# Two-layer hybrid encoder on one Trainium2 core: the first feed-forward product of 19 of 22 column pairs as seven products of quarters, with all sums of weights on VectorE

## The chip, the cores and the metric

The kernel runs on one core of a Trainium2 chip. The core has a matrix engine (TensorE, PE in the profile; PEld is its weight load), a vector engine (VectorE, DVE), a scalar engine (ScalarE, ACT), a general one (GpSimd, POOL) and a queue that issues transfers (SyncE, SP). The engines run side by side, each its own list of instructions in order, and wait for each other by semaphores. The metric is the device time of one execution in microseconds. Each kernel is timed in several runs, and the median counts.

## What is computed

Two layers of an encoder over 512 tokens with 1024 features in float32. Each layer mixes the tokens with four kinds of mixers (gated linear attention, neighbourhood attention, a linear recurrence, dilated attention) and then applies a gated feed-forward part of width 2816:

```python
for l in range(DEPTH):                       # DEPTH = 2
    h = rmsnorm(x, mix_norm_pre[l])
    p = h @ w_in[l]
    ...                                      # four mixers on slices of p, joined to y (512 x 1024)
    x = x + rmsnorm(y, mix_norm_post[l])
    h = rmsnorm(x, ffn_norm_pre[l])
    gate, up = jnp.split(h @ ffn_w_in[l], 2, axis=-1)        # 1024 x 5632 weights
    f = (jax.nn.silu(gate) * up) @ ffn_w_out[l]              # 2816 x 1024 weights
    x = x + rmsnorm(f, ffn_norm_post[l])
```

The change concerns `h @ ffn_w_in[l]` alone, the first feed-forward product.

## The kernel before, in words

**Products.** TensorE multiplies in a rounded float32 format. To keep float32 precision every operand is split into a high part (a cast, `wh` for weights) and a low part (the rest, `wl`), and `mm3` (L357) issues three matmuls into one accumulator: high by high, high by low, low by high. For the first feed-forward product the weights are the stationary operand, so the first two share `wh`, the third takes `wl`, and the activations stream, 512 columns (tokens) at a time.

**The first feed-forward product**, `ffn_in` (L1288). The 5632 output features are 22 column pairs: pair i holds 128 gate features and the 128 up features that belong to them. Pairs 0 to 2 (`NP`) are run by `parts` in two cuts of 256 tokens, so that they can start while the later tokens are still being normalised. Pairs 3 to 21 are run one after the other: for each of the two banks (a `d` bank for gate, an `x` bank for up) `mpart` (L628) issues 8 chunks of the 1024 features, three matmuls of 512 columns each, so 48 matmuls per pair. When both banks are done, `ffn_act` (L1303) makes Silu(gate) on ACT, the multiplication by up on DVE, a cast on ACT and a low part on DVE; the result `f[i]` is two tiles of 128x512, in the form the second product wants.

**The second product**, `ffn_out` (L1317), goes over k = 0 to 21 in order and uses `f[k]` and one tile of weights each, with 12 matmuls of 512 columns.

**Weights.** `w_load` (L407) walks through all weights in the order of use (`stream`, L388). It issues the transfers on SP and starts a `w_split` (L425) for each half tile: a cast on ACT and a low part on DVE or POOL, whichever is free first by the builder's reckoning. `w_get` (L442) hands them to the products in the order of use. At most four split tiles (`NW`) of this kind exist at a time; the other tiles come from a pool of 74 (`NM`, named `m`).

**What sets the order.** The program is built by a planner (`go`, L318). Every piece of work is a Python generator that yields the engine it needs next ("P", "A", "V", "G", "D"). The planner keeps a clock for each engine, advances the piece that could start first (then by the number given as its priority), and adds a modelled cost. What it emits is a fixed list of instructions for each engine. On the chip an engine runs its list in that order, so an instruction that must wait holds up all behind it on its engine, even those whose inputs are there.

All instructions of the profile below have line L187, that of the helper that records them.

Of the kernel before, what the change touches and what calls it, by code (L numbers as in the profile page):

```python
# [15 lines left out]
P = 128  # L16
L = 512
# [21 lines left out]
CUTS = ((0, 256), (256, 512))  # L39
NV = 44  # L40
# [101 lines left out]
class Timed:  # L142
# [5 lines left out]
    def __getattr__(self, name):  # L148
# [47 lines left out]
       "VP": 77, "GG": 60, "GV": 60, "GA": 75, "GP": 60}  # L196

# [7 lines left out]
class Builder:  # L205
# [151 lines left out]
    def mm3(self, out, a, b, first=True, last=True):  # L357

        mm = self.pe.matmul
        mm(out, a[0], b[0], start=first, stop=False)  # L360
        mm(out, a[0], b[1], start=False, stop=False)
        mm(out, a[1], b[0], start=False, stop=last)
# [25 lines left out]
    def stream(self):  # L388
        d = self.d
        for l in range(self.depth):  # L390
            for i in range(W2_AT):
                yield d["w1"][l, i], "m" if NW // 2 <= i < NF else "w"
            for i in range(KD // 2):
                yield d["w2"][l, i], "w"
            for i in range(W2_AT, 20):
                yield d["w1"][l, i], "w"
            for h in range(2):
                for i in range(KD // 2):
                    yield d["wo"][l, h, i], "wm"[h]
            for i in range(KF):  # L400
                for j in range(2):
                    yield d["wf1"][l, i, j], "m" if NW // 2 <= 2 * i + j < 2 * NP else "w"
            for h in range(2):
                for i in range(KF // 2):
                    yield d["wf2"][l, h, i], "m" if h and 2 * i >= KF - TAIL else "w"

    def w_load(self):  # L407
        for i, (src, kind) in enumerate(self.stream()):
# [12 lines left out]
            for h in range(2):  # L421
                self.spawn(self.w_split(2 * i + h, half[h], kind, "" if k == "s" and h == 0 else k),
                           1 if i > 2 else i - 2.5)
# [61 lines left out]
    def pre_half(self, t, i, r, gi, h, ok, keep):  # L485
# [15 lines left out]
        for k, src, g in part:  # L501
            self.act.activation(h[0][k][:, ts], src, AF.Copy, scale=g)
        yield "V"
        for k, src, g in part:
            self.dve.scalar_tensor_tensor(h[1][k][:, ts], src, g, h[0][k][:, ts].bitcast(F32), ALU.mult, ALU.subtract)
# [122 lines left out]
    def mpart(self, h, bank, c0=0, c1=L, w=None):  # L628

        new = not w  # L630
        for k in range(KD):
            if new and k % 4 == 0:
                a = yield from self.w_get()
                if w is not None:
                    w.append(a)
            elif not new:
                a = w[k // 4]
            s = slice((k % 4) * P, (k % 4) * P + P)
            if k % 2 == 0:
                yield "P"  # L640
            self.mm3(bank[:, c0:c1], (a[0][:, s], a[1][:, s]), (h[0][k][:, c0:c1], h[1][k][:, c0:c1]),
                     k == 0, k == KD - 1)
            if k % 4 == 3 and (w is None or c1 == L):
                self.give(*a[2:])
# [78 lines left out]
    def z_proj(self, l, h, st):  # L723
# [4 lines left out]
        for k in range(KD):  # L728
            if k % 2 == 0:
                yield "P"  # L730
            if k:
                self.pe.matmul(b[0:32], w[:, k * 64:k * 64 + 32], h[1][k], start=False, stop=False)
            self.pe.matmul(b[0:64], w[:, k * 64:(k + 1) * 64], h[0][k], start=k == 0, stop=k == KD - 1)
            if k == 0:
                self.pe.matmul(b[0:32], w[:, 0:32], h[1][0], start=False, stop=False)
# [13 lines left out]
    def v_proj(self, l, h, st):  # L749
# [3 lines left out]
        for k in range(KD):  # L753
            w = yield from self.w_get()
            for t in range(NT):
                if t % 2 == 0:
                    yield "P"
                a = (h[0][k][:, t * P:(t + 1) * P], h[1][k][:, t * P:(t + 1) * P])
# [460 lines left out]
    def new_h(self):  # L1219
        return [self.m(F32R) for _ in range(KD)], [self.m(F32R) for _ in range(KD)]  # L1220

# [65 lines left out]

    def ffn_in(self, l, h, ok, f):  # L1288
# [3 lines left out]

        yield from self.parts(h, ok, "dx" * NP, CUTS, done)
        for i in range(NP, KF):
            b = []
            for n in "dx":
                b.append((yield from self.acq(n)))
            for n in range(2):
                yield from self.mpart(h, b[n])
            self.spawn(self.ffn_act(i, b, f), 2)  # L1300
        self.give("m", 16)
# [54 lines left out]
    def dense(self):  # L1356
        h, ok = self.h0, self.ok0
        yield from self.need(16, 0)
        for l in range(self.depth):
# [7 lines left out]
            h, ok = self.new_h(), []  # L1367
# [6 lines left out]
            h, ok = (self.new_h(), []) if l < self.depth - 1 else (None, None)  # L1374
# [3 lines left out]
    def build(self):  # L1378
        nc = self.nc
        self.wnext, self.wuse, self.wrdy, self.nk_ok, self.c_ok = 0, 0, {}, False, False  # L1380
# [16 lines left out]
        self.h0, self.ok0 = self.new_h(), []  # L1397
# [56 lines left out]
```

## Time and profile before

| what | value |
| --- | --- |
| time, median of 3 runs | 1270.73 us (1269.66 to 1271.34) |
| the profiled execution: its time, its span | 1267.58 us, 1265.8 us |
| granted TensorE clock, mean over the span | 0.998 |
| PE busy | 1242.6 us, 98% |
| DVE busy | 582.9 us, 46% |
| ACT busy | 557.0 us, 44% |
| POOL busy | 192.9 us, 15% |
| mean DMA rate | 99 GB/s |
| products of pairs 3 to 21, first layer | 309.91 to 516.66 us of the span |
| the same, second layer | 933.17 to 1139.92 us of the span |

The span goes from the first to the last instruction that the profiler saw; the execution's time has some 2 us around it. The profiled execution is one of its own, 3 us below the median of the timed runs. Matmuls in the timeline are pipelined: a group of them shows a longer duration than the distance from its start to the next group's start, and it is that distance that counts. The same holds for DVE and ACT, with a smaller difference.

### The profile page before, as it was taken

What the parts mean: (1) busy time and instruction counts of PE and PEld (TensorE: products, weight loads), DVE (VectorE), ACT (ScalarE), POOL (GpSimd) and SP (SyncE); (2) the same over time, 40 slices, a digit from 0 to 9 for tenths busy, and PEclk for the clock granted to TensorE, in tenths of its full rate; (3) what the DMA queues carried; (4) which work ended last, traced back from release to release, by engine and by line L of the source; (5) the groups of instructions that cost most, each with busy time, mean ns of one, the idle gap of its engine ahead of it and who ended that gap; (6) DMA issues with size and microseconds to landing.
All of it is one profiled execution on the core that took longest, in us unless ns stands there. A gap on an engine that the chain in (4) does not pass through costs nothing.

```text
span 1265.8 us, 17216 instructions
## 1 busy us (share of the span) xinstructions
PE 1242.6 (98%) x6538; PEld 1023.0 (81%) x6538; DVE 582.9 (46%) x1174; ACT 557.0 (44%) x1181; POOL 192.9 (15%) x175
## 2 busy tenths in 40 slices
PE   8999999999999999999999899999999999999998
PEld 7876777789888888888897777778998888888886
DVE  6477765572333232212465868656633332332222
ACT  6476755563333333223448555555533333332230
POOL 5011111230110111111230111112211011111120
PEclk9999999999999999999999999999999999999999
DMA  7413151424020123334460311613241111333331
GB/s 238 169 55 112 34 175 59 166 86 165 17 84 9 44 82 100 117 94 142 164 213 1 125 59 40 211 34 133 84 141 58 35 67 34 100 105 102 110 117 67
DMA packets 55619, 124.97 MB, mean 99 GB/s; under 512 B 6640, under 2 KB 7024, under 8 KB 55536
## 3 DMA queue, kind: packets, MB, share of 16 engines
q1 hardware_dynamic: 55248, 123.34, 29.7%
q8 instruction: 51, 0.84, 0.3%
q10 hardware_dynamic: 288, 0.52, 0.1%
q14 instruction: 32, 0.26, 0.1%
HBM read 117.55 MB, written 4.19 MB: 96 GB/s over the span
## 4 chain that ended last, share of the span: by engine, by line
PE 88%; DVE 6%; ACT 3%; issue 2%; DMA 1%; POOL 0%; SPq 0%; DVEq 0%; POOLq 0%; ACTq 0%
PE bx L187 47%; PE bd L187 41%; DVE m L187 5%; ACT m L187 3%; DVE wl L187 1%; DMA ws<-in_w 0%; ACT wh L187 0%; ACT L187 0%; POOL s L187 0%; DMA m<-in_wf 0%; POOL wl L187 0%; DVE s L187 0%; SPq L352 0%; DVE sbd L187 0%; DVE att L187 0%
## 5 line engine op out<-in xcount | busy, mean ns | idle before, releaser
L187 PE MATMUL bd<-m,wh 128*128 128x512 f32 (+1 forms) x1248 | 366.2, 377 | 1.1 <-ACT m L187 1.1
L187 PEld LDWEIGHTS bd<-m,wh 128*128 128x128 f32 x1248 | 224.4, 188 | 45.3 <-issue 5.2
L187 PE MATMUL bx<-m,m 128*128 128x256 f32 (+6 forms) x1616 | 247.0, 345 | 6.6 <-DVE m L187 6.1
L187 PE MATMUL bd<-m,wl 128*128 128x512 f32 (+1 forms) x624 | 233.1, 374 | 0.0
L187 PEld LDWEIGHTS bx<-m,m 128*128 128x128 f32 (+2 forms) x1616 | 184.9, 176 | 58.6 <-issue 21.0
L187 ACT CAST wh<-ws 128x512 fp32r<-128x512 f32 x162 | 100.5, 621 | 261.7 <-PE bx L187 192.4
L187 ACT CAST wh<-m 128x512 fp32r<-128x512 f32 x166 | 102.9, 620 | 228.5 <-PE bx L187 105.9
L187 PE MATMUL bx<-m,wh 128*128 128x512 f32 (+1 forms) x672 | 198.9, 379 | 0.0
L187 DVE TENSOR_TENSOR wl<-ws,wh 128x512 fp32r<-128x512 f32 x115 | 80.6, 700 | 250.1 <-ACT wh L187 250.0
L187 DVE TENSOR_TENSOR wl<-m,wh 128x512 fp32r<-128x512 f32 x119 | 84.8, 713 | 230.6 <-ACT wh L187 228.2
L187 PE MATMUL bd<-wh,m 128*128 128x512 f32 x424 | 144.8, 392 | 0.0
L187 PEld LDWEIGHTS bx<-m,wh 128*128 128x128 f32 x672 | 124.1, 188 | 23.6
L187 PE MATMUL bx<-wh,m 128*128 128x512 f32 x408 | 138.4, 390 | 0.0
L187 PEld LDWEIGHTS bd<-m,wl 128*128 128x128 f32 x624 | 117.5, 188 | 21.2
L187 POOL TENSOR_TENSOR wl<-ws,wh 128x512 fp32r<-128x512 f32 x47 | 60.6, 1289 | 459.1 <-ACT wh L187 423.4
L187 POOL TENSOR_TENSOR wl<-m,wh 128x512 fp32r<-128x512 f32 x47 | 61.5, 1308 | 451.0 <-ACT wh L187 401.5
L187 PE MATMUL bx<-m,wl 128*128 128x512 f32 (+1 forms) x336 | 127.3, 379 | 0.0
L187 DVE TENSOR_TENSOR m<-m,m 128x512 fp32r<-128x512 f32 (+2 forms) x116 | 83.3, 725 | 48.2 <-ACT m L187 48.0
L187 PEld LDWEIGHTS bd<-wh,m 128*128 128x128 f32 x424 | 79.6, 188 | 17.6 <-issue 0.9
L187 PEld LDWEIGHTS bx<-wh,m 128*128 128x128 f32 x408 | 76.6, 188 | 16.3 <-issue 0.2
L187 ACT CAST m<-m 128x512 fp32r<-128x512 f32 (+1 forms) x100 | 60.3, 618 | 58.0 <-DVE m L187 58.0
L187 PE MATMUL bd<-wl,m 128*128 128x512 f32 x212 | 82.5, 389 | 0.0
(100 smaller groups left out, 1210.8 us busy)
## 6 DMA issues: line engine op xcount, KB each, us to landing
ws<-in_wf SPq DMA_DIRECT2D x70, 512.0 KB, 3.5
m<-in_wf SPq DMA_DIRECT2D x124, 256.0 KB, 4.8
m<-in_w SPq DMA_DIRECT2D x64, 256.0 KB, 5.0
ws<-in_w SPq DMA_DIRECT2D x16, 512.0 KB, 3.6
m<-in_wo SPq DMA_DIRECT2D x24, 256.0 KB, 3.9
m<-in_x SPq DMA_DIRECT2D x14, 256.0 KB, 5.6
m<-in_rpb SPq DMA_DIRECT2D x12, 256.0 KB, 4.0
m<-m SPq DMA_DIRECT2D x32, 64.0 KB, 2.0
```

Source lines behind the costliest of these rows:

```text
L187: return f(out, *a, **k)
```

## The change

A pair's weights are 1024 x 256. The change reads a pair as a product of 2 x 2 blocks: the features in two halves, the columns as gate and up, the tokens as two halves of 256. Instead of eight block products it computes seven, by Winograd's form of Strassen's method, each of them 4 chunks x 3 matmuls of 256 columns, 84 in all. It does so for pairs 3 to 21; pairs 0 to 2 stay as they are.

What it adds: `h` is stored in halves of tokens (`Halved`). `h_forms` makes four sums of activation blocks for each of four chunks, once per layer: 12 operations on DVE and 4 on ACT of 128x256 per chunk. `pair_load` loads a pair's weights as four tiles a, b, c, d of 256 KB and starts `sums` and a `form` (cast on ACT, low part now always on DVE) for each of the seven weight blocks. With `SUMS = "V"` the four sums e = c + d, c + a, a + e, b + a run on DVE. `pair_side` combines the products beside the accumulation in PSUM: ACT copies products 1 and 5, DVE makes two sums, then come Silu and the multiplications in halves of 128x256. `f` of a pair stays one tile until all products are issued; then `f_conv` makes the two tiles that the second product wants (`self.conv`). Of the functions that only changed their names for parts of `h` (`mpart`, `z_proj`, `v_proj`, `pre_half`) nothing is shown.

```diff
+    def sums(self, q):
+        n = q["n"]
+        add = lambda o, a, b: self.dve.tensor_tensor(q[o], q[a], q[b], ALU.add)
+        if SUMS == "V":
+            yield lambda: {"c", "d", "e0"} & n >= {"c", "d"}
+            yield "V"
+            add("e", "c", "d")
+            n.add("e")
+            yield lambda: "a.split" in n
+            yield "V"
+            add("c", "c", "a")
+            n.add("c1")
+        yield lambda: "a.split" in n and "e" in n
+        yield "V"
+        add("a", "a", "e")
+        n.add("a2")
+        yield lambda: "e.split" in n
+        self.give("m")
+        yield lambda: "b.split" in n
+        yield "V"
+        add("b", "b", "a")
+        n.add("b2")
...
+    def prod(self, dst, n, hf, fresh):
+        w = yield from self.w_get()
+        for k in range(KD // 2):
+            s, t = slice(k * P, (k + 1) * P), hf[n, k]
+            if k % 2 == 0:
+                yield "P"
+            self.mm3(dst, (w[0][:, s], w[1][:, s]), (t[:, 0:HALF], t[:, HALF:L]), fresh and k == 0, k == 3,
+                     skip_group_check=True)
+        self.give(*w[2:])
+    def pair_side(self, b, q, f, i):
+        u0, g1, g0, u1 = b[0][:, 0:HALF], b[0][:, HALF:L], b[1][:, 0:HALF], b[1][:, HALF:L]
+        yield lambda: 1 in q
+        yield "A"
+        self.act.copy(u0, g0)
+        q.add("u0")
+        yield from self.need(2, 0)
+        e, a = self.m(), self.m()
+        yield lambda: 5 in q
+        yield "A"
+        self.act.copy(e[:, 0:HALF], u1)
+        yield lambda: 6 in q
+        yield "V"
+        self.dve.tensor_tensor(g1, u0, e[:, 0:HALF], ALU.add)
+        q.add("g1")
+        yield lambda: 7 in q
+        yield "V"
+        self.dve.tensor_tensor(e[:, HALF:L], u0, e[:, 0:HALF], ALU.add)
+        q.add("u1")
+        yield lambda: 2 in q
+        yield "A:Silu"
+        self.act.activation(a[:, 0:HALF], g0, AF.Silu)
+        self.give("x")
+        yield lambda: 3 in q
+        yield "A:Silu"
+        self.act.activation(a[:, HALF:L], g1, AF.Silu)
+        yield "V"
+        self.dve.tensor_tensor(a[:, HALF:L], a[:, HALF:L], e[:, HALF:L], ALU.mult)
+        self.give("m")
+        yield lambda: 4 in q
+        yield "V"
+        self.dve.tensor_tensor(a[:, 0:HALF], a[:, 0:HALF], u0, ALU.mult)
+        self.give("d")
+        self.spawn(self.f_conv(i, a, f), 1)
+    def f_conv(self, i, a, f):
+        yield lambda: self.conv
+        yield from self.need(2, 0)
+        o = self.mr2()
+        yield "A"
+        self.act.activation(o[0], a, AF.Copy, scale=-1.0)
+        yield "V"
+        self.dve.scalar_tensor_tensor(o[1], a, -1.0, o[0].bitcast(F32), ALU.mult, ALU.subtract)
+        self.give("m")
+        f[i] = o
...
+        yield lambda: l in self.forms_ok
+        self.give("m", 4)
+        old = None
+        for i in range(NP, KF + 1):
+            new = None
+            if i < KF:
+                self.pnow = i
+                b = []
+                for n in "dx":
+                    b.append((yield from self.acq(n)))
+                new = (b[1][:, 0:HALF], b[0][:, HALF:L], b[0][:, 0:HALF], b[1][:, HALF:L], set())
+                self.spawn(self.pair_side(b, new[4], f, i), 0)
+            for who, n, at, wait in ((new, 1, 0, 0), (new, 5, 3, 0), (old, 4, 2, "u1"), (new, 6, 2, "u0"),
+                                     (old, 3, 1, "g1"), (new, 2, 0, 0), (new, 7, 2, "g1")):
+                if who:
+                    if wait:
+                        yield lambda: wait in who[4]
+                    yield from self.prod(who[at], n, hf, n == 1)
+                    who[4].add(n)
+            old = new
+        self.conv = True
+        self.give("m", 28)
```

The last piece stands in `ffn_in`, behind the call of `parts` for pairs 0 to 2; `h_forms` is spawned ahead of that call.

**What moves, at three places.** The first is the joint between two of the pairs in the first layer. On DVE of the changed kernel, the rows from the sum g1 of the old pair on: b + a of its weights, the two multiplications of the pair before it, u1 (which waits for product 7), then for the new pair e = c + d, the low part of a, c + a, and the low part of e:

```order
L191 TENSOR_TENSOR bd818_3766<-bd818_3766,m825_3803 128x256
L191 TENSOR_TENSOR m813_3711<-m813_3711,m794_3628 128x512
L191 TENSOR_TENSOR m803_3667<-m803_3667,m802_3666 128x256
L191 TENSOR_TENSOR m803_3667<-m803_3667,bd791_3624 128x256
L191 TENSOR_TENSOR m825_3803<-bd818_3766,m825_3803 128x256
L191 TENSOR_TENSOR m837_3886<-m820_3771,m827_3806 128x512
L191 TENSOR_TENSOR wl840_3889<-m815_3750,wh839_3888 128x512
L191 TENSOR_TENSOR m820_3771<-m820_3771,m815_3750 128x512
L191 TENSOR_TENSOR wl845_3912<-m837_3886,wh844_3911 128x512
```

On PE of the changed kernel at that joint, the end of product 7 (into the `d` bank 818) and the first matmuls of the new pair's product 1, with `wh` and `wl` of its a:

```order
L191 MATMUL bd818_3766<-m765_3508,m834_3814 128x256 x2
L191 MATMUL bd818_3766<-m765_3508,m835_3815 128x256
L191 MATMUL bx842_3904<-m563_2472,wh839_3888 128x256 x2
L191 MATMUL bx842_3904<-m563_2472,wl840_3889 128x256
L191 MATMUL bx842_3904<-m565_2474,wh839_3888 128x256 x2
L191 MATMUL bx842_3904<-m565_2474,wl840_3889 128x256
L191 MATMUL bx842_3904<-m567_2476,wh839_3888 128x256 x2
```

And on DVE of the kernel before, in the same stretch, two pairs' worth: low parts of weights (`wl`), the multiplication by up and the low part of f:

```order
L187 TENSOR_TENSOR m821_3723<-m821_3723,bx803_3643 128x512
L187 TENSOR_TENSOR m825_3743<-m821_3723,m824_3742 128x512
L187 TENSOR_TENSOR wl828_3763<-m745_3252,wh827_3762 128x512
L187 TENSOR_TENSOR wl830_3779<-m756_3355,wh829_3778 128x512
L187 TENSOR_TENSOR wl834_3797<-m757_3356,wh833_3796 128x512
L187 TENSOR_TENSOR m835_3798<-m835_3798,bx818_3720 128x512
L187 TENSOR_TENSOR m839_3818<-m835_3798,m838_3817 128x512
```

What moved: between u1, which reads product 7, and the low part of a there is now one sum, e, and that low part is what the third matmul of the product directly behind product 7 takes. Before, the multiplication of a pair also stood ahead of a low part of weights (the third row, `wl828`), but PE took that tile as the sixth one behind the pair's last bank (`bx803`); the first, `wl808`, was made on POOL.

The second place is the end of `h_forms` in the first layer, on DVE of the changed kernel. The first row is the multiplication of pair 2, which reads the last bank of the second cut (`bx733`); the third is the low part of its f; the last two are e and the low part of a for pair 3:

```order
L191 TENSOR_TENSOR m755_3476<-m755_3476,bx733_3242 128x512
L191 TENSOR_TENSOR m756_3479<-m748_3399,m756_3479 128x256
L191 TENSOR_TENSOR m758_3484<-m755_3476,m757_3483 128x512
L191 SCALAR_TENSOR_TENSOR m759_3486<-m746_3397,m759_3486 128x256
L191 TENSOR_TENSOR m760_3491<-m746_3397,m760_3491 128x256
L191 TENSOR_TENSOR m761_3494<-m569_2478 128x256
L191 TENSOR_TENSOR m761_3494<-m578_2487 128x256
L191 TENSOR_TENSOR m762_3495<-m570_2479 128x256
L191 TENSOR_TENSOR m762_3495<-m577_2486 128x256
```

```order
L191 TENSOR_TENSOR m763_3496<-m761_3494,m762_3495 128x256 x2
L191 TENSOR_TENSOR m761_3494<-m763_3496,m761_3494 128x256
L191 TENSOR_TENSOR m761_3494<-m761_3494,m762_3495 128x256
L191 TENSOR_TENSOR m764_3505<-m763_3496,m764_3505 128x256
L191 TENSOR_TENSOR m765_3508<-m763_3496,m765_3508 128x256
L191 SCALAR_TENSOR_TENSOR m766_3511<-m761_3494,m766_3511 128x256
L191 TENSOR_TENSOR m767_3514<-m761_3494,m767_3514 128x256
L191 TENSOR_TENSOR m774_3527<-m771_3521,m772_3523 128x512
L191 TENSOR_TENSOR wl777_3530<-m768_3517,wh776_3529 128x512
```

The same place before, from the multiplication of pair 2 to the next low parts of weights:

```order
L187 TENSOR_TENSOR m768_3478<-m768_3478,bx746_3267 128x512
L187 TENSOR_TENSOR m772_3492<-m768_3478,m771_3491 128x512
L187 TENSOR_TENSOR wl778_3522<-m633_2722,wh777_3521 128x512
L187 TENSOR_TENSOR wl780_3538<-m649_2765,wh779_3537 128x512
L187 TENSOR_TENSOR wl786_3560<-m650_2766,wh785_3559 128x512
```

What moved: fifteen half-wide operations of `h_forms` (the row with the mark x2 is two), the low part of f and the sum e now stand between the multiplication of pair 2 and the first low part of pair 3; before, only the low part of f did.

The third place is the end of the pairs in the first layer, on ACT of the changed kernel: the last Silu (reading a `d` bank), then the copies of `f_conv`, of which the last rows are shown too, and the cast of a tile of second-product weights:

```order
L191 CAST wh1209_6098<-ws1187_5961 128x512
L191 ACTIVATE m1193_5995<-bx1186_5958 128x256
L191 CAST wh1211_6117<-ws1200_6009 128x512
L191 ACTIVATE m1193_5995<-bd1185_5957 128x256
L191 ACTIVATE m1238_6160<-m788_3568 128x512
```

```order
L191 ACTIVATE m1268_6190<-m1125_5585 128x512
L191 ACTIVATE m1270_6192<-m1148_5722 128x512
L191 CAST wh1272_6194<-ws1200_6009 128x512
L191 ACTIVATE m1274_6196<-m1171_5859 128x512
L191 CAST wh1282_6230<-ws1213_6119 128x512
```

What moved: 17 copies of f stand in a row between the last Silu and that cast; before, each pair's copy stood beside the pair's own products.

## Rows read from the trace of the kernel before

**Rows 1.** The page: busy time, chain that ended last, DMA issues.
```profile
PE 1242.6 (98%) x6538; PEld 1023.0 (81%) x6538; DVE 582.9 (46%) x1174; ACT 557.0 (44%) x1181; POOL 192.9 (15%) x175
...
PE 88%; DVE 6%; ACT 3%; issue 2%; DMA 1%; POOL 0%; SPq 0%; DVEq 0%; POOLq 0%; ACTq 0%
...
m<-in_wf SPq DMA_DIRECT2D x124, 256.0 KB, 4.8
```

**Rows 2.** Windows; columns: us, then busy us (count) per engine, PEclk, DMA share, GB/s.
```profile
309.91:516.66 206.75, 206.75 (x915) 171.18 (x913) 63.40 (x94) 67.28 (x112) 24.48 (x19) 1.00 0.21 66
933.17:1139.92 206.75, 206.75 (x914) 171.18 (x913) 63.49 (x94) 67.28 (x112) 24.48 (x19) 1.00 0.21 66
```

**Rows 3.** Waits of PE; columns: engine line, waited for: total us, times, longest.
```profile
PE bx L187 <- DVE m L187: 13.9, 12, 4.0
```

**Rows 4.** Timeline of PE, second cut to pair 3 (start us, us, engine, operation).
```profile
307.03 3.04 PE L187 MATMUL bx<-m,m 128*128 128x256 f32 x24
309.91 0.63 PE L187 MATMUL bd<-m,wh 128*128 128x512 f32 x2
```

**Rows 5.** Timeline of DVE: third multiplication and low part of f; middle of the products.
```profile
310.18 0.69 DVE L187 TENSOR_TENSOR m<-m,bx 128x512 f32<-128x512 f32 x1 [3.69 <-PE bx L187]
311.56 0.69 DVE L187 TENSOR_TENSOR m<-m,m 128x512 fp32r<-128x512 f32 x1 [0.69 <-ACT m L187]
...
430.29 0.69 DVE L187 TENSOR_TENSOR wl<-m,wh 128x512 fp32r<-128x512 f32 x1 [2.03 <-ACT wh L187]
430.90 0.68 DVE L187 TENSOR_TENSOR m<-m,bx 128x512 f32<-128x512 f32 x1
```

**Rows 6.** Operations of DVE by form (busy us, mean ns | idle before, releasers).
```profile
L187 DVE TENSOR_TENSOR wl<-m,wh 128x512 fp32r<-128x512 f32 x30 | 20.8, 693 | 69.0 <-ACT wh L187 69.0
...
L187 DVE TENSOR_TENSOR m<-bx,m 128x256 fp32r<-128x256 f32 x16 | 6.8, 424 | 26.0 <-ACT m L187 26.0
L187 DVE TENSOR_TENSOR m<-m,m 128x256 fp32r<-128x256 f32 x2 | 0.8, 414 | 0.0
```

**Rows 7.** Timeline of ACT, and one of its operations by form.
```profile
275.75 0.67 ACT L187 CAST m<-m 128x512 fp32r<-128x512 f32 x1
276.26 1.20 ACT L187 CAST m<-ws 128x512 fp32r<-128x512 f32 x2
...
307.29 0.60 ACT L187 ACTIVATE m<-bd 128x512 f32<-128x512 f32 x1 [1.53 <-PE bd L187]
...
L187 ACT CAST m<-bx 128x256 fp32r<-128x256 f32 x16 | 5.9, 368 | 12.1 <-PE bx L187 12.0
```

**Rows 8.** Operations of POOL by form, stretch 310 to 516.
```profile
L187 POOL TENSOR_TENSOR wl<-m,wh 128x512 fp32r<-128x512 f32 x10 | 12.9, 1289 | 102.2 <-ACT wh L187 92.6 <-DMA m<-in_wf 9.6
```

**Rows 9.** Gaps of PE and the clock behind them: timelines, then windows.
```profile
95.84 0.72 PE L187 MATMUL bd<-m,wh 128*128 128x512 f32 x2 [1.13 <-ACT m L187]
...
105.60 1.16 PE L187 MATMUL bx<-m,m 64*128 64x128 f32 x16 [1.29 <-DVE m L187]
106.69 0.66 PE L187 MATMUL bx<-ident,m 128*128 128x128 f32 x4
...
719.29 1.28 DVE L187 TENSOR_TENSOR m<-m,m 128x512 f32<-128x512 f32 x2
...
720.11 1.76 PE L187 MATMUL bx<-m,m 64*128 64x128 f32 x16 [4.04 <-DVE m L187]
721.81 1.11 PE L187 MATMUL bx<-ident,m 128*128 128x128 f32 x4
722.85 1.65 PE L187 MATMUL bx<-m,m 64*128 64x128 f32 x16
...
721.00:722.00 1.00, 1.00 (x10) 0.78 (x8) 0.32 (x2) 0.00 (x0) 0.00 (x0) 0.50 0.46 127
...
723.00:724.00 1.00, 1.00 (x10) 1.00 (x12) 1.00 (x2) 0.00 (x0) 0.00 (x0) 0.55 0.76 252
724.00:725.00 1.00, 1.00 (x15) 0.88 (x12) 0.76 (x3) 0.00 (x0) 0.00 (x0) 1.00 0.91 307
```

More of the change, by code (lines that the diff above doesn't have):

```diff
@@ L39 @@
 CUTS = ((0, 256), (256, 512))
+HALF = 256
+SUMS = "V"
+ROOM = 3
+FROOM = 6
 NV = 44
@@ L399, in stream @@
                     yield d["wo"][l, h, i], "wm"[h]
-            for i in range(KF):
+            for i in range(NP):
                 for j in range(2):
                     yield d["wf1"][l, i, j], "m" if NW // 2 <= 2 * i + j < 2 * NP else "w"
+            for i in range(NP, KF):
+                yield (l, i), "pair"
             for h in range(2):
@@ L407, in w_load @@
     def w_load(self):
-        for i, (src, kind) in enumerate(self.stream()):
+        n = 0
+        for src, kind in self.stream():
+            if kind == "pair":
+                yield from self.pair_load(*src, n)
+                n += 7 if src[1] > NP else 5
+                n += 2 if src[1] == KF - 1 else 0
+                continue
             yield lambda: self.tok["s"] or len(self.tok["m"]) >= 2 + STAGE
@@ new lines, in add_load @@
+    def add_load(self, q, name, src):
+        yield "G"
+        self.nc.gpsimd.dma_start(q[name], src, accum_op=ALU.add)
+        self.cost += 1000.0
+        self.moved = max(self.moved, self.start + self.cost + 650.0) + 262144 / 180.0
+        self.cur.after = self.moved + 1500.0
+        yield "V"
+        q["n"].add(name)
+        self.cost = 0.0
+    def sums(self, q):
+        n = q["n"]
+        add = lambda o, a, b: self.dve.tensor_tensor(q[o], q[a], q[b], ALU.add)
+        if SUMS == "V":
+            yield lambda: {"c", "d", "e0"} & n >= {"c", "d"}
[16 more added lines that the diff above has]
+        n.add("b2")
+        yield lambda: "a2.split" in n
+        self.give("m")
@@ new lines, in form @@
+    def form(self, i, q, name):
+        n = q["n"]
+        src = name[0]
+        have = "c1" if SUMS == "V" and name == "c" else name
+        yield lambda: self.wnext == i and have in n and (self.tok["w"] or len(self.tok["m"]) >= 2 + FROOM)
+        self.wnext += 1
+        if self.tok["w"]:
+            self.take("w")
+            w = (self.whp.tile([P, 512], F32R, tag="wh", name=self.nm("wh")),
+                 self.wlp.tile([P, 512], F32R, tag="wl", name=self.nm("wl")), "w", 1)
+        else:
+            self.take("m", 2)
+            w = (*self.mr2(), "m", 2)
+        yield from self.split(w[:2], q[src], "V")
+        n.add(name + ".split")
+        if name in ("c", "d", "b2"):
+            self.give("m")
+        self.wrdy[i] = w
@@ L1291, in done @@
                 self.spawn(self.ffn_act(i // 2, b[i - 1:i + 1], f), 2)
+        hf = {}
+        self.conv, self.pnow = False, NP
+        self.spawn(self.h_forms(l, h, ok, hf), 2)
         yield from self.parts(h, ok, "dx" * NP, CUTS, done)
[L1294 to L1301, printed above, removed]
+        yield lambda: l in self.forms_ok
[20 more added lines that the diff above has]
+        self.give("m", 28)
     def ffn_act(self, i, b, f):
```

128 lines of the change are left out of this document (109 added, 19 removed).

## Prediction

> **What bounds the kernel now.** I read the busy shares first: TensorE (PE) is busy in 1242.6 of the 1265.8 us of the span, and the chain of waits that ended last is 88% PE [rows 1]. The stretches of the two layers' feed-forward products say the same more sharply: the 19 column pairs 3 to 21 take 206.75 us in either layer, PE is busy in all of it, and VectorE (DVE) in 63.40 of it [rows 2]. So PE sets the time there. 19 pairs of 48 matmuls are 912, hence 0.2267 us for one of 512 columns. PE's list of waits shows hardly anything to win elsewhere: 13.9 us in twelve waits for DVE, the longest 4.0 [rows 3]. DVE could carry more work on average. What decides is at which place in its order that work stands, since each engine executes the order that the builder wrote.
>
> **The change, part by part. The matmuls** that it removes and adds: a pair costs seven products of 12 matmuls of 256 columns, 84, instead of 48 of 512. Matmuls of that shape, with the same change of weights, run in pairs 0 to 2 already: 24 from 307.03 to 309.91 [rows 4], 0.120 us each. 84 x 0.120 = 10.08 us against 48 x 0.2267 = 10.88; over 19 pairs 191.5 against 206.75: **-15.2 us per layer**, if PE waits for nothing. This is the whole gain: one multiplication of eight is saved (12.5%), but the half-wide matmul costs 53% of the wide one, so only 7% is left.
>
> Weighed against a rule: 0.120 for 256 columns and 0.2267 for 512 are what the rows show. The Trainium skill, "TensorE: Matmul & The Clock Gate", section "Back-to-back issue gap", gives 262 cycles (109 ns) and 518 cycles (215.8 ns) instead. By it a pair would save 10.36 - 9.17 = 1.19 us, 45 us in all instead of 30, and the time would be some 15 us lower than my forecast. The page and the rows differ, and the measurement decides.
>
> **VectorE's work per pair**: four sums and seven low parts of 128x512, two sums and two multiplications of 128x256. One after the other, DVE's 128x512 operations start 0.61 us apart (430.29 to 430.90), though each shows 0.69 [rows 5]; the half-wide ones show 0.41 to 0.42 [rows 6], so with the same 0.08 of overlap I take them 0.34 apart. 11 x 0.61 + 4 x 0.34 = 8.1 us of 10.08: it fits, with 2 us to spare. ScalarE (ACT) has seven casts at 0.52 apart (275.75 to 276.26) and four half-wide operations of 0.37 [rows 7], some 5 us: it fits too. The weights of a pair are four transfers of 256 KB; such ones land 4.8 us after issue [rows 1], and the stretch uses 0.21 of the DMA engines' time [rows 2]: hidden.
>
> **The joint between two pairs.** The order shows, at every one of the 18 joints of a layer, on DVE: sum u1 of the old pair, which waits for the last matmul of its product 7; then e = c + d of the next pair; then the low part of that pair's a. On PE product 1 of the next pair stands directly behind product 7, and its third matmul wants that low part. So the low part, which could have been made any time since its weights landed, is queued behind a wait for PE's own last matmul. Step by step from that matmul's end: PE to DVE 0.27 (PE's stage ends at 309.91, DVE starts at 310.18) [rows 4, 5]; u1 0.34; e 0.61; low part 0.69 to its end (a 128x512 one on this engine, thirty in the stretch at 693 ns) [rows 6]; DVE to PE 0.14 (DVE's first of two operations that start at 719.29 ends near 719.97 at 0.68, PE starts at 720.11) [rows 9]. That is 2.05. Two matmuls of product 1 run ahead, 0.24: 1.81. After a gap the first two matmuls of a group show 0.72 instead of 0.62 [rows 9], so I take **1.85 us**, 18 x 1.85 = **+33.3 per layer**. Lower end: low part 0.61 and no slower start: 1.59 x 18 = 28.6. Upper end: u1 0.42, e 0.69 and the slower start whole: 2.07 x 18 = 37.3. Inside a pair I find no wait of that kind: the low part of a2 comes about 0.4 before its product, the ACT copy u0 falls into product 5. This is near; 0 to 0.15 a pair, 0 to 2.9 a layer, stands in the upper bound only.
>
> **The start.** The twelve forms of activations per k-group, 48 half-wide operations on DVE, stand between the last norm of the mixing part and the first low part of pair 3. They are tangled with the three multiplications of pairs 0 to 2, and the third of these waits for the end of PE's second cut, 309.91. DVE starts it at 310.18 and, with its wait for the cast, the low part of f at 311.56 [rows 5] (one form fits into that wait); then 0.61 for it, 14 forms x 0.34 = 4.76, e 0.61, low part of a 0.69, to PE 0.14: 318.37. Product 1's third matmul is due at 309.91 + 0.24 = 310.15: **8.2 us** of idle PE. Before, PE went through this instant without a gap [rows 4]. After its one long gap in the trace, 4.04 us, the clock stood at 0.50 (1.2 GHz) for the following stage, 0.55 in the microsecond 723 to 724 and 1.00 from 724 on; its first three groups took 1.76, 1.11 and 1.65 us, where groups of the same form at full clock take 1.16, 0.66 and 1.16 [rows 9]. That is 1.5 longer, some of it spent in waits of that stage, so I add 1.2: **+9.4** (6 if DVE slips forms into its waits, 12 if the clock is worse and ACT is late).
>
> **The end.** Products 4 and 3 of the last pair have nothing ahead of them: product 4 waits for u1, 0.27 + 0.42 + 0.14 = 0.83. Then 24 x 0.12 = 2.88, so they end 3.71 after product 7. The Silu reads that at +0.26 (307.03 to 307.29) [rows 4, 7], about 4.3 when it is done. Behind it on ACT stand 17 deferred copies of f, 17 x 0.52 = 8.84, and only then the cast of the fourth tile of second-product weights: 13.1, with its 0.62 13.7; its low part is on POOL, 1.29 [rows 8], about 15.1, and at PE 15.2. PE reaches it after 36 matmuls, 36 x 0.2267 = 8.16, and 0.3 for a bank that the Silu still reads, with the first matmul of the tile: 12.4. It waits 2.9. **0.83 + 0.3 + 2.9 = +4.0** (2.5 to 6). In the kernel before these copies are made as each pair ends, under PE.
>
> **The sum.** -15.2 + 33.3 + 9.4 + 4.0 = +31.5 us per layer; both layers have the same order at these places, +63.0. The profiled execution took 1267.58 us (span 1265.8 and 1.8 around it): 1330.6. It lies 3.15 under the median of the runs shown, 1270.73, so the forecast is 1333.7, **1334 us**. Lower bounds of all terms: -15.2 + 28.6 + 6 + 2.5 = 21.9, twice 43.8: 1314. Upper: -15.2 + 37.3 + 12 + 6 + 2.9 = 43.0, twice 86: 1357.
>
> **The rivals.** First, the *clock follows the joints*. A gap of 1.85 us every 12 is between the ones that the trace has: 1.13 (ahead of 95.84) and 1.29 (ahead of 105.60) left the next matmuls at 0.62 and 0.66, full speed; 4.04 halved the clock [rows 9]. If each of the 36 joints also cost what the long gap did, 1.2 us, the sum grows by 43: 1377. The Trainium skill speaks for it: "TensorE: Matmul & The Clock Gate", section "A second HAM failure mode: psum-queue depth-cycling", says that repeated small idles between matmul groups can make the gate swing. Against it is that the three gaps of one microsecond here cost nothing, and 1.85 is nearer to these. Chance 0.09.
>
> Second, and on the other side, *TensorE stays bound*: DVE's low part of a gets done ahead of need, because its wait on product 7 is shorter than I read or its time lies under product 1. Speaks for it: DVE has 8.1 us of work for 10.08. The joints then cost nothing, and start and end stay: -15.2 + 9.4 + 4.0 = -1.8 per layer, 1267; with start and end hidden too -15.2, 1240. The point from which it decides: with start and end as I have them, a joint may cost 0.1 us for the change to break even, (15.2 - 13.4) / 18; with these hidden, 0.84. Against it: u1 can't start before product 7 ends, and e and the low part stand behind it in DVE's order at all 36 joints. Chance 0.05.
>
> That the change doesn't do what it says is no case: the order of PE has the 84 matmuls of 128x256 in each of the pairs.
>
> **How the numbers follow.** Forecast (slower by 44 to 86 us) 0.86, clock rival 0.09, TensorE bound 0.05. The range is the forecast's own, 1314 to 1357; the two rivals, 0.14, lie outside. 0.2% (2.5 us) is about what a measurement of this kernel can tell from no change. Slower: 0.86 + 0.09 = 0.95. Of the last rival's 0.05, 0.04 is faster and 0.01 the same.
>
> **What would show it.** In the changed kernel's stretch of products: PE idle about 1.8 us ahead of the third matmul of every product 1, released by DVE on the low part; 18 such waits a layer, and matmuls of 0.120 between them; one wait of about 8 us at the first, with the clock at 0.50 behind it; one of about 3 us in the first tiles of the second product, released by POOL; DVE's u1 0.27 behind PE's last matmul of product 7. The list of PE's waits should hold some 65 us for DVE in place of 13.9. Wrong would be: joints under 0.9 us; a wait for casts or transfers in the place of these; a granted clock under 1.00 through the whole stretch; or half-wide matmuls that take over 0.13.

## The result, and the profile after

The changed kernel takes **1371.88 us** (median of four runs, 1369.74 to 1374.29), the kernel before 1271.03 us (median of four, 1269.66 to 1271.49): a ratio of 1.0796, interval 1.077 to 1.0822. The forecast was 1334 with a range of 1314 to 1357. The direction was right; the loss is 38 us larger than forecast and lies above the range.

The profiled execution took 1373.97 us, its span is 1372.2. The busy line of its page (engine, busy us, share of the span, instructions) and the list of what PE waited for (engine line, waited for: total us, times, longest) are:

```profile
PE 1246.8 (91%) x7906; PEld 1079.1 (79%) x7906; DVE 829.3 (60%) x1688; ACT 650.8 (47%) x1441; POOL 152.7 (11%) x137
```

```profile
PE bx L191 <- DVE wl L191: 54.8, 38, 1.5
PE bx L191 <- ACT bd L191: 17.1, 38, 0.5
PE bx L191 <- DVE m L191: 16.1, 11, 4.0
PE bx L191 <- ACT wh L191: 13.5, 2, 6.8
PE bd L191 <- POOL wl L191: 10.6, 2, 5.3
PE bd L191 <- ACT wh L191: 4.1, 4, 1.4
```

Before, PE was busy 98% and its list held one entry of weight, 13.9 us for DVE [rows 1, 3]. That entry is still there (16.1). Five are new, and each belongs to a place of the program: 38 waits for DVE's `wl` (36 joints with 1.48 us each, and one of 0.73 at the start of the products in each layer), 38 for ACT's `bd` (a copy inside each pair), 2 for ACT's `wh` (the start again), and 2 for POOL and 4 for ACT at the end. PE's busy time hardly changed, although it has fewer columns to run: a half-rate clock is part of it. The windows of after (us; busy us and count of PE, PEld, DVE, ACT, POOL; granted clock; DMA share; GB/s) show where:

```profile
312.09:560.67 248.58, 205.28 (x1598) 197.05 (x1597) 166.82 (x302) 104.26 (x218) 1.28 (x1) 0.97 0.22 75
320.00:328.00 8.00, 6.95 (x31) 6.66 (x32) 4.14 (x7) 2.84 (x6) 0.00 (x0) 0.50 0.11 35
345.00:545.00 200.00, 169.43 (x1344) 162.93 (x1344) 134.10 (x241) 84.10 (x176) 0.00 (x0) 1.00 0.24 80
577.00:580.00 3.00, 3.00 (x8) 2.31 (x7) 0.00 (x0) 0.00 (x0) 0.00 (x0) 0.50 0.79 285
```

The first row is the stage of pairs 3 to 21: 248.58 us against 206.75 [rows 2], 41.8 more. The third has the middle of that stage: the clock is 1.00 through its sixteen joints, and PE is busy in 85%. The second and the fourth are at half clock: behind the start, and in the second product.

**A joint and a pair's middle**, about 432 and 436 us, in the timeline of all engines (start us, us, engine, operation, and in brackets the idle time before it and its releaser):

```profile
431.80 0.40 PE L191 MATMUL bx<-m,wh 128*128 128x256 f32 x2
432.01 0.42 DVE L191 TENSOR_TENSOR m<-bd,m 128x256 f32<-128x256 f32 x1 [1.71 <-PE bd L191]
432.35 0.68 DVE L191 TENSOR_TENSOR m<-m,m 128x512 f32<-128x512 f32 x1
432.94 0.68 DVE L191 TENSOR_TENSOR wl<-m,wh 128x512 fp32r<-128x512 f32 x1
...
433.68 0.38 PE L191 MATMUL bx<-m,wl 128*128 128x256 f32 x1 [1.48 <-DVE wl L191]
...
435.57 0.28 PE L191 MATMUL bx<-m,wl 128*128 128x256 f32 x1
435.89 0.36 ACT L191 COPY bd<-bx 128x256 f32<-128x256 f32 x1 [1.63 <-PE bx L191]
...
436.30 0.50 PE L191 MATMUL bx<-m,wh 128*128 128x256 f32 x2 [0.45 <-ACT bd L191]
```

The joint is as forecast, operation by operation: DVE's u1 at 432.01 waits for product 7 of the old pair, then come e and the low part of a, and PE's third matmul of product 1 starts at 433.68. Without the wait it would start at 431.80 + 0.24 = 432.04. So the wait costs 1.64, and the matmul behind it takes 0.22 to 0.23 to the next instead of 0.12: 1.74 a joint. Four microseconds on stands what I had put at nothing. Product 5 is half done (its sixth matmul starts at 435.57), the ACT copy of product 1 runs from 435.89 to 436.25, and only behind it does the seventh matmul start, 0.73 later instead of 0.12. With the slower restart (the two matmuls from 436.30 take 0.34 to the next, not 0.24) that is 0.70 to 0.71 a pair. A whole pair takes 12.516 us = 10.08 + 1.74 + 0.70.

**The start**, PE's timeline and, in the second fence, DVE's. PE's second cut ends at 309.21 + 24 x 0.12 = 312.09:

```profile
309.21 3.04 PE L191 MATMUL bx<-m,m 128*128 128x256 f32 x24
319.02 0.79 PE L191 MATMUL bx<-m,wh 128*128 128x256 f32 x2 [6.77 <-ACT wh L191]
320.55 0.58 PE L191 MATMUL bx<-m,wl 128*128 128x256 f32 x1 [0.73 <-DVE wl L191]
...
328.80 0.40 PE L191 MATMUL bx<-m,wh 128*128 128x256 f32 x2
...
331.67 0.40 PE L191 MATMUL bx<-m,wh 128*128 128x256 f32 x2
```

```profile
300.84 0.69 DVE L191 TENSOR_TENSOR m<-m,bx 128x512 f32<-128x512 f32 x1 [2.26 <-PE bx L191]
...
306.60 0.69 DVE L191 TENSOR_TENSOR m<-m,bx 128x512 f32<-128x512 f32 x1 [4.74 <-PE bx L191]
...
312.36 0.69 DVE L191 TENSOR_TENSOR m<-m,bx 128x512 f32<-128x512 f32 x1 [2.19 <-PE bx L191]
```

In the midst of the forms DVE stands still 2.26 + 4.74 + 2.19 = 9.2 us for the three multiplications of pairs 0 to 2, and ends the forms after PE has run out of work. PE's first wait there (6.77) is for ACT's cast of pair 3's a, which stands behind four copies of the last forms, and these wait for DVE; the second (0.73) is for DVE's low part. From 312.09 to the first matmul of the second pair at 331.67 pass 19.58 us. The 60 matmuls there take 7.2 at full clock and the pair's middle 0.71, so the start cost 11.7: 6.9 idle, 0.7 in the second wait, and 4.0 since 36 matmuls ran at half clock (0.213 apart instead of 0.120 makes 3.4 of them).

**The end**, the timelines of ACT, DVE, POOL and PE one after the other. The second product starts at 560.67:

```profile
561.15 8.96 ACT L191 ACTIVATE m<-m 128x512 fp32r<-128x512 f32 x17
570.01 0.61 ACT L191 CAST wh<-ws 128x512 fp32r<-128x512 f32 x1
```

```profile
561.96 10.92 DVE L191 SCALAR_TENSOR_TENSOR m<-m,m 128x512 fp32r<-128x512 f32 x18
572.80 1.28 DVE L191 TENSOR_TENSOR wl<-ws,wh 128x512 fp32r<-128x512 f32 x2
...
574.61 0.68 DVE L191 TENSOR_TENSOR wl<-m,wh 128x512 fp32r<-128x512 f32 x1
```

```profile
570.70 5.71 POOL L191 TENSOR_TENSOR wl<-ws,wh 128x512 fp32r<-128x512 f32 x1 [13.07 <-ACT wh L191]
```

```profile
570.67 0.50 PE L191 MATMUL bd<-wh,m 128*128 128x512 f32 x1 [1.44 <-ACT wh L191]
576.46 0.79 PE L191 MATMUL bd<-wl,m 128*128 128x512 f32 x1 [5.29 <-POOL wl L191]
...
581.32 0.40 PE L191 MATMUL bd<-wh,m 128*128 128x512 f32 x1
```

ACT reaches the cast of the fourth tile at 570.01. That is 13.05 after the end of product 7 (556.96), where I had 13.1. But POOL's low part, 1.29 us before [rows 8], now takes 5.71: it ends 1.1 us after DVE's unbroken row of operations ends at 575.29. PE waits 1.6 for the cast and 5.6 for the low part, and then runs at half clock. The first four tiles took 20.65 us (560.67 to 581.32); 48 matmuls at 0.2267 are 10.88: +9.8. The wait of product 4 for u1 (556.96 to 557.73) adds 0.8.

| us per layer | forecast | measured |
| --- | --- | --- |
| products, 84 half-wide matmuls for 48 | -15.2 | -15.2 |
| 18 joints | +33.3 (1.85 each) | +31.3 (1.74 each) |
| 19 pairs' middles | 0 (0 to 2.9) | +13.3 (0.70 each) |
| start | +9.4 (6 to 12) | +11.7 |
| end | +4.0 (2.5 to 6) | +10.6 (0.8 + 9.8) |
| sum | +31.5 | +51.7 |

The second layer takes as long, from the end of its second cut to its fifth tile of second-product weights 269.2 us as in the first. Two layers make 103.4 of the 106.4 between the spans. The other 3.0 lie mostly ahead of pair 3 of the first layer: a group of 24 matmuls in the middle of the first cut starts at 279.00 before and at 281.06 here. That is a difference between executions and not the change, since in the kernels run below the same group starts between 278.81 and 281.22.

### The profile page after: what moved, and what is told of

It reads as the page before. It is cut to its first block, busy times and chain, and to the rows that moved or that the text cites. A ratio compares the mean times of both kernels' runs of the same rounds, so it can differ in the third digit from the quotient of the medians.

```text
span 1372.2 us, 20926 instructions
## 1 busy us (share of the span) xinstructions
PE 1246.8 (91%) x7906; PEld 1079.1 (79%) x7906; DVE 829.3 (60%) x1688; ACT 650.8 (47%) x1441; POOL 152.7 (11%) x137
## 5 line engine op out<-in xcount | busy, mean ns | idle before, releaser
L191 PE MATMUL bd<-m,wh 128*128 128x256 f32 (+1 forms) x1680 | 370.8, 316 | 2.3 <-ACT wh L191 1.2
L191 PE MATMUL bx<-m,m 128*128 128x256 f32 (+7 forms) x1928 | 289.5, 336 | 6.6 <-DVE m L191 6.1
L191 PEld LDWEIGHTS bd<-m,wh 128*128 128x128 f32 x1680 | 274.3, 192 | 23.3 <-issue 6.7
L191 DVE TENSOR_TENSOR wl<-m,wh 128x512 fp32r<-128x512 f32 x277 | 188.2, 697 | 155.3 <-ACT wh L191 154.8
L191 PE MATMUL bd<-m,wl 128*128 128x256 f32 (+1 forms) x840 | 262.9, 313 | 0.0
L191 ACT CAST wh<-m 128x512 fp32r<-128x512 f32 x302 | 181.7, 619 | 164.9 <-DVE m L191 61.7
L191 DVE TENSOR_TENSOR m<-m,m 128x512 f32<-128x512 f32 (+3 forms) x372 | 228.1, 628 | 47.8 <-ACT m L191 47.4
L191 PE MATMUL bx<-m,wh 128*128 128x256 f32 x768 | 151.7, 294 | 30.5 <-ACT bd L191 17.1
L191 PE MATMUL bx<-m,wl 128*128 128x256 f32 x384 | 114.5, 298 | 54.8 <-DVE wl L191 54.8
L191 PEld LDWEIGHTS bx<-m,wl 128*128 128x128 f32 x384 | 75.2, 196 | 62.7 <-DVE wl L191 62.7
L191 PE MATMUL bd<-wl,m 128*128 128x512 f32 x212 | 84.4, 398 | 10.6 <-POOL wl L191 10.6
```

Of the source, the lines that this page charges most:

```text
L191: return f(out, *a, **k)
```

## The experiments

The theory after the comparison is: the place of a few instructions in their engine's row makes the whole loss, in four separate places, and the work that the change adds isn't its cause. The rivals: DVE's added work (829 us busy for 583) or the clock under 36 short idles sets the time; then moving an instruction moves the wait to another place and gains little. Seven kernels each change one of these places, an eighth four of them. Each gain is against 1371.88. Beside these runs the kernel before took 1270.1 and 1271.57 (medians of seven), so a gain is good to some 2 us.

**The copy inside a pair.** `pair_side` releases the copy u0 when product 1 is done, and its reading of that bank's one half was put between the matmuls of product 5, which write the other half. In this kernel the copy is released after product 5:

```diff
     def pair_side(self, b, q, f, i):
...
-        yield lambda: 1 in q
+        yield lambda: 5 in q
         yield "A"
         self.act.copy(u0, g0)
...
-        yield lambda: 5 in q
         yield "A"
         self.act.copy(e[:, 0:HALF], u1)
```

> One edit to the changed kernel: ACT's copy of product 1 (u0) waits for the end of product 5 as well, so it no longer stands between the halves of product 5, which writes the same bank. Queue theory (each wait is one instruction's place in its engine's list): the stop in the middle of product 5, 0.61 us and 0.10 for the late weight load behind it, 38 times, goes: 27 us less than the changed kernel, about 1345. Load theory (VectorE and ScalarE have too much to do in a pair, and a wait that is taken away comes back at the next place): product 6 needs the copy and waits instead, within 5 us of 1372.

Measured: **1346.43 us**, ratio to before 1.0597 (1.0579 to 1.0616), 25.5 less. Of PE's 38 waits for ACT's `bd` two of 0.5 are left, now ahead of product 6 in the first pair of each layer, where no product of an old pair stands between; its 38 waits for DVE are there as before:

```profile
PE bx L191 <- DVE wl L191: 54.8, 38, 1.5
...
PE bd L191 <- ACT bd L191: 1.0, 2, 0.5
```

So PE waited for no value, since the copy reads one half of the bank and product 5 writes the other; it waited since the program keeps a reader and the writers of one bank in order, wherever the builder sets the reader. Whether both could go on at once, no run here tries. 25.5 / 38 = 0.67 each.

**The joint, first way.** In the builder's plan `pair_load` issues its four transfers in separate steps. The plan lets each wait for the landing of the one before, 2.9 us as it reckons, 11.6 for four: more than the pair's 10.08 us of matmuls. In this kernel they are issued in two steps:

```diff
-        for name, first, more in order:
-            yield lambda: len(self.tok["m"]) >= 1 + ROOM
-            self.take("m", 1)
-            q[name] = self.m()
-            if first:
-                yield "D"
-                self.dma(q[name], src[first], 262144)
...
+        for part in (("c", "d"), ("a", "b", "e")):
+            yield lambda: len(self.tok["m"]) >= len(part) + ROOM
...
+            yield "D"
+            for name in part:
+                if name in src:
+                    self.dma(q[name], src[name], 262144)
...
```

> One edit to the changed kernel: the four transfers of a pair's weights are issued in two steps of the builder's plan (c and d, then a and b) instead of four; instructions and their numbers stay the same, only the order of the lists changes: e = c + d and the low part of a then stand ahead of u1 on VectorE. Queue theory: the wait at the joint, 1.64 us and 0.10 behind it, 36 times, goes: 62 us less, about 1309. Load theory: VectorE has the same work in each pair, the joints stay or move, within 10 us of 1372.

Measured: **1306.73 us**, ratio 1.0282 (1.0263 to 1.0302), 65.2 less. Of 38 waits for DVE's `wl` the two at the starts are left, and 34 of the 38 stops inside the pairs stay:

```profile
PE bx L191 <- ACT bd L191: 15.3, 34, 0.5
...
PE bx L191 <- DVE wl L191: 1.5, 2, 0.7
```

The added work is all still there, on the same engine. The joints were its place, and its place came from the plan's picture of the transfers: with the same transfers, issued in two steps (c and d first), the joints are gone. 36 joints of 1.74 and four stops of 0.70 make 65.4.

**The joint, second way.** Here the transfers are left alone, and `form` and `sums` are started ahead of them instead of behind the last (the block of `spawn` lines moved above the loop).

> One edit to the changed kernel: casts, low parts and sums of a pair are known to the builder before its four transfers are issued, not after the last of them. In the lists the low part of a then stands ahead of u1, but e = c + d still stands behind u1. Queue theory: product 1 no longer waits, but product 5, whose weights are e, does: sum 0.61, cast and low part behind u1, less the 1.44 of product 1, about 1.8 us a pair in place of 1.64 + 0.61 (the copy u0 lies under that wait): some 20 us less than the changed kernel, about 1351. If the low part of a alone were the cause, it would be 62 us less, 1309. Load theory: within 10 us of 1372.

Measured: **1347.08 us**, ratio 1.0605 (1.0589 to 1.0621), 24.8 less: a bit over a third of the other way. The waits did not go, they moved; the first fence is PE's list of waits, the second its timeline:

```profile
PE bx L191 <- ACT wh L191: 50.8, 40, 6.8
...
PE bx L191 <- DVE wl L191: 8.1, 36, 0.2
```

```profile
427.72 0.28 PE L191 MATMUL bx<-m,wl 128*128 128x256 f32 x1
428.98 0.50 PE L191 MATMUL bx<-m,wh 128*128 128x256 f32 x2 [0.98 <-ACT wh L191]
429.71 0.38 PE L191 MATMUL bx<-m,wl 128*128 128x256 f32 x1 [0.23 <-DVE wl L191]
```

Product 1 now has its low part in time; product 5, twelve matmuls on, waits for e, its cast and its low part. e still stands late, since the plan still has its inputs landing late. A pair takes 11.80 us (one between such waits, 417.18 to 428.98) in place of 12.516: the new wait is as dear as the joint, and the gain is the stop of the copy, which now lies under it.

**Fewer sums on DVE.** The builder's other setting makes e and c + a by accumulating transfers (`SUMS = "V"` becomes `"G"`), which takes 76 operations off DVE.

> One part of the change undone: e = c + d and c + a are made by transfers that add into the tile, issued by POOL, so VectorE has two sums of 128x512 less in each pair. Queue theory: one operation of 0.61 us less between u1 and the low part of a, 36 joints: 22 us less than the changed kernel, about 1350. Load theory: VectorE is relieved of 2 x 0.61 in every pair, 46 us less, about 1326. If the adding transfers land late: over 1372.

Measured: **1350.92 us**, ratio 1.0644 (1.0623 to 1.0666), 21.0 less. DVE's busy time falls to 784.5, and each joint loses about the 0.61 of e that stood in it, and no more:

```profile
PE bx L191 <- DVE wl L191: 31.9, 36, 1.0
```

The 36 joints had 53.3 of the 54.8, so (53.3 - 31.9) / 36 = 0.60 a joint. Taking 45 of DVE's 246 added us off it gains a third of what its order gains.

**The end, paced.** The deferred copies of `f` are released only up to five ahead of the second product, instead of all at once:

```diff
     def f_conv(self, i, a, f):
 
-        yield lambda: self.conv
+        yield lambda: self.conv and i < self.fk + 5
...
             for k in range(KF):
+                self.fk = max(self.fk, k)
```

> One edit to the changed kernel: the deferred copies of f are released as the second product comes near them (five ahead) instead of all at once, so casts of weights stand between them. In the changed kernel TensorE waits 1.6 and 5.6 us at the first tiles of the second product and runs some 2.4 us longer at half clock behind it. Queue theory with a shared port (POOL's low part took 5.7 us, because VectorE ran without a pause beside it): both waits and the clock's loss go, about 9 us per layer: 18 us less than the changed kernel, 1354. If POOL's 5.7 us are its own price there: some 3 us per layer for ACT's queue alone, 1366.

Measured: **1353.74 us**, ratio 1.0646 (1.0618 to 1.0673), 18.1 less. PE's waits for POOL are gone, and the same low part on POOL takes 1.30 again. The timelines of POOL and DVE:

```profile
564.61 1.30 POOL L191 TENSOR_TENSOR wl<-ws,wh 128x512 fp32r<-128x512 f32 x1 [6.95 <-ACT wh L191]
```

```profile
565.10 1.36 DVE L191 SCALAR_TENSOR_TENSOR m<-m,m 128x512 fp32r<-128x512 f32 x1 [0.61 <-ACT m L191]
```

Here POOL had started first, and it is DVE's operation that is long: 1.36 for 0.69.

**The end, POOL's part alone.** The copies stay in a row, but the low parts of the six weight tiles behind the pairs are made on DVE, so that none is on POOL.

> One edit to the changed kernel: for the six tiles of weights behind the end of the pairs the low part is made on VectorE, none on POOL; the 17 copies stay in one row. The low part then stands behind 18 low parts of f on VectorE. Shared-port theory: TensorE gets it where VectorE is done with these, near 573.6 on the time axis of the changed kernel, against 576.5 from POOL: 2.9 us per layer, 6 less, 1366; the clock still falls. If VectorE's row were not what POOL waited for, the low part would come earlier than that: 1360 or less, or, if VectorE is the tighter queue, over 1372.

Measured: **1365.27 us**, ratio 1.0744 (1.0725 to 1.0763), 6.6 less. The low part now stands behind 17 operations in DVE's row. Timelines of DVE and PE:

```profile
558.09 10.31 DVE L191 SCALAR_TENSOR_TENSOR m<-m,m 128x512 fp32r<-128x512 f32 x17
568.32 0.68 DVE L191 TENSOR_TENSOR wl<-ws,wh 128x512 fp32r<-128x512 f32 x1
```

```profile
566.79 0.50 PE L191 MATMUL bd<-wh,m 128*128 128x512 f32 x1 [1.43 <-ACT wh L191]
569.06 0.50 PE L191 MATMUL bd<-wl,m 128*128 128x512 f32 x1 [1.76 <-DVE wl L191]
...
571.52 0.63 PE L191 MATMUL bx<-wh,m 128*128 128x512 f32 x1
571.95 0.63 PE L191 MATMUL bx<-wl,m 128*128 128x512 f32 x1
```

PE waits 1.76 for it instead of 5.29 for POOL: 3.5 less per layer, 7.0 for two, and the gain is 6.6. So the choice of POOL behind this row is some 3.5 of the end's 9.8, and the rest goes only with the row itself, as the paced kernel shows: with either engine the clock still falls behind the waits (the last two rows are 0.43 apart, at full clock 0.2267).

**The start.** The Silu, the multiplication and the low part of pairs 0 to 2 are released only when the forms are done, and the low part after that of pair 3's a:

```diff
     def ffn_act(self, i, b, f):
...
+        yield lambda: self.l0 in self.forms_ok
         yield "A:Silu"
...
+        yield lambda: 'a.split' in self.pairs.get((self.l0, NP), {'n': ()})['n'] if i == NP - 1 else self.l0 in self.forms_ok
         yield "V"
         self.dve.tensor_tensor(a, a, b[1], ALU.mult)
         self.give("x")
+        yield lambda: 'a.split' in self.pairs.get((self.l0, NP), {'n': ()})['n']
```

> One edit to the changed kernel: Silu, multiplication and low part of pairs 0 to 2 are released only when the forms of the activations are made (and, for the last multiplication and the low parts, when the first weights of pair 3 are split), so VectorE and ACT don't wait for TensorE's cuts in the middle of the forms. Queue theory: the first wait (6.9 us), the one on its third matmul (1.0) and the half clock behind them (3.4 and 0.3) go, 11.7 us per layer: 23 less than the changed kernel, 1348. Load theory (48 half-wide operations don't fit under the two cuts): half of it or less, 1360 to 1372.

Measured: **1351.1 us**, ratio 1.0635 (1.0613 to 1.0656), 20.8 less. The waits of the two starts are gone, and the stretch behind the start is at full clock (a window again):

```profile
311.00:330.00 19.00, 16.80 (x132) 15.79 (x131) 14.55 (x26) 8.06 (x17) 0.00 (x0) 1.00 0.25 76
```

**All four.** The copy after product 5, the transfers in two steps, the paced copies and the cleared start, together.

> The four edits together: transfers in two steps, copy u0 behind product 5, paced copies of f, start cleared. The number and kinds of instructions are the changed kernel's. Queue theory: 1372 less 65 (as measured for the transfers), 25 (the copy), 18 and 23: about 1243, which is faster than the kernel before (1270) by about 2%; what is left of the 30 us that the seven products save then shows, 191.5 us per layer for the 19 pairs plus small rests. Load theory: one of the engines becomes the bound, 1270 or more.

Measured: **1245.64 us** (1243.63 to 1246.55) against 1271.57 for the kernel before on the same chip: a ratio of **0.9802** (0.9783 to 0.9821). It beats both kernels. The four gains alone are 25.5 + 65.2 + 18.1 + 20.8 = 129.6, which would give 1242.3: they add up nearly, and four stops inside pairs, some 2.8 us, are counted in two of them. The busy line of the page, the largest of PE's waits (the twelve that were there before too; none other for DVE or ACT is over 1.2 us in total), and the window of pairs 3 to 21 in the first layer:

```profile
PE 1213.6 (98%) x7906; PEld 1064.0 (86%) x7906; DVE 838.8 (68%) x1686; ACT 653.7 (53%) x1441; POOL 147.1 (12%) x139
```

```profile
PE bx L191 <- DVE m L191: 16.2, 12, 4.1
```

```profile
310.84:504.50 193.66, 192.33 (x1599) 191.72 (x1597) 161.60 (x286) 102.03 (x210) 1.29 (x1) 1.00 0.29 92
```

Two of after's low parts went from DVE to POOL here; otherwise the instructions are as many. The stage takes 193.66 us against 206.75 before [rows 2]; 19 x 10.08 is 191.5. DVE is busy in 83% of it and PE waits for it hardly at all. So DVE's added work was not the bound. Of the 30.4 us that the seven products save in two layers the kernel has 25.9.

## Why the prediction was right in part, and where it failed

**Right: the direction, the gain and the joints.** Half-wide matmuls stand 0.120 apart, so the products give 15.2 a layer, as worked out. The joint's chain (u1, e, low part) is in the trace in that order, and measured 1.74 for 1.85. DVE's three operations held (1.61 from 432.01 to 433.62, for 1.64); the passing from engine to engine was quicker (0.21 for 0.27 from PE, 0.06 for 0.14 to PE) and the restart a little slower (0.10 for 0.04). The forecast's lower end of the joint, 1.59, is added up wrongly: its terms make 1.73, and the range would begin at 1319. The waits at the joints were forecast at some 65 us in PE's list; it has 53.3, as it counts 1.48 of the 1.64.

**Failed, the largest: a pair's middle.** The step is "Inside a pair I find no wait of that kind: ... the ACT copy u0 falls into product 5", priced at "0 to 0.15 a pair". The place was read rightly and the consequence wrongly. I asked whether the copy is in time for its own readers, and not whether the matmuls behind it in the same bank may go on. In this program they may not: 0.70 x 38 = 26.6 us, and undoing it gave back 25.5. That is the larger part of the miss.

**Failed, the end.** The step is "its low part is on POOL, 1.29". The row of the cast was right within 0.05 us, the duration behind it wrong: 5.71 beside DVE's unbroken row of low parts. And I gave the end no clock term, although PE stands idle 5.6 us in one piece there, longer than the 4.04 of [rows 9]. 10.6 for 4.0, so 13.2 in two layers.

**Mis-sized, the start.** DVE's row was right: I had the third matmul of product 1 at 8.2 behind its due time, and it started at 320.55 for 312.33. That PE stands two matmuls earlier already, for ACT's cast, I did not see; it adds nothing to the wait, since DVE's low part comes later still. The clock term was taken as 1.2 from a stage that was back at full clock 3.9 us after its gap [rows 9]; here half clock lasted from 319.02 to about 328.8. 3.5 for 1.2, 4.6 in two layers. A part of that is the luck of the execution: behind the same idle time the seven kernels that keep this start (the changed one and six of those above) were at half clock for 4.4 to 10.4 us. In the kernel with low parts on DVE PE starts again at 316.90 in the first layer and at 990.21 in the second, and its windows show both cases:

```profile
322.00:323.00 1.00, 0.66 (x5) 0.66 (x6) 0.14 (x1) 1.00 (x3) 0.00 (x0) 1.00 0.00 0
...
991.00:1000.00 9.00, 7.77 (x35) 7.46 (x35) 5.08 (x9) 2.92 (x6) 0.00 (x0) 0.50 0.09 31
```

Together 26.6 + 13.2 + 4.6 - 4.0 (joints) = 40.4, and 3.0 outside the products: the 43.4 between the profiled execution's 1373.97 and the 1330.6 forecast for one. The range failed with the middle's upper bound, 2.9 a layer for 13.3, and with the end's.

**The rivals.** That the clock follows the joints is refuted: 1.00 through 200 us with sixteen of them. The Trainium skill, "TensorE: Matmul & The Clock Gate", section "A second HAM failure mode: psum-queue depth-cycling", tells that repeated small idles can make the gate swing; at 1.5 us of idle every 12.5, the trace here doesn't show it. Against this rival I counted three gaps of a microsecond in the kernel before; its rows show two, 1.13 and 1.29 [rows 9]. That TensorE stays bound is refuted for this kernel, and reached by the eighth one with the same arithmetic: my lower ends of it, 1267 and 1240, were times of another order of the same work, and 1245.64 lies between them.

## What to carry to other kernels

When a kernel runs fixed rows of instructions, sum the waits at each place where one engine's row crosses another's, and count both sides of every shared bank: not only who needs the reader's result, but which writers stand behind it. A planner's reckoning of transfers decides places too (here it put 1.3 us of work behind a wait that it had no part in, at each of 36 joints), and work put off to the end comes back as a burst ahead of what the next stage needs; releasing it at the pace of its readers gave back 18 us with no less work.

## What the runs showed of the hardware

- An operation of POOL that takes 1.29 us [rows 8] took 5.71 while DVE ran two-input operations without a pause, and ended 1.1 us after the last of them, so nearly all of its own time lay behind them. The other way round, with POOL first, DVE's 0.69 became 1.36. The Trainium skill, "SBUF — State Buffer", section "Who interferes with whom", says that such a pair contends for a shared read port and that the order of issue decides who blocks; both rows agree with that.
- The clock after an idle stretch: 6.9 us of idle were followed by half clock for 4.4 to 10.4 us from the restart (14 starts in seven kernels; 9.8 in both of the changed kernel's), 4.04 us by 3.9 [rows 9], and joints with 1.5 us of idle by none: the granted clock was 1.00 through sixteen of them.
- The first matmul behind a late weight tile takes 0.22 to 0.23 us to the next one instead of 0.12 (433.68 to 433.91).
